# Four pieces of x on the scalar queue, six weight chunks loaded early into lent space, and high-part products first

## The chip, the cores and the metric

One NeuronCore of a Trainium2 chip runs the whole program in one launch. The metric is the device time of one execution in microseconds (us), as the median of several runs. Engines are named as the profile names them: PE is TensorE's matrix multiplication and PEld its weight load, DVE is VectorE, ACT is ScalarE, POOL is GpSimd, SP is SyncE, whose queue issues most of the transfers.

## What is computed

Two layers of a decoder trunk over 256 tokens of 1024 numbers, all in float32. Only the start of the first layer matters here:

```
def hybrid_layer(x, ...):
    h = rms_norm(x, attn_pre_gain)
    u = h @ w_in                      # 1024 -> 4120 columns
    qa, ka, va, qb, kcb, vcb, ksb, vsb, kwb, vwb, g_nsa, g_a, g_b = split(u)
    ...                               # two kinds of attention, merged
    x = x + rms_norm(mixed @ w_out, attn_post_gain)
    h = rms_norm(x, ffn_pre_gain)
    x = x + rms_norm(conv_ffn(h, ...), ffn_post_gain)
```

## The kernel before, in words

Every float32 matrix product is made of three products of a reduced type (float32r). A number is split into a high part (ScalarE copies and rounds it, `copy`, L114) and a low part (VectorE subtracts the high part from the number, `sub`, L117), and `mm3` (L365 to L368) multiplies high by high (L366), high of x by low of the weight (L367) and low of x by high of the weight (L368), all three into one PSUM bank. The row factor of the RMS norm is applied to the result, so products can run before it is known; the gain is multiplied into x.

The weights come as a stream of chunks in the order of their use (`Stream`, L145). `load` allots a staging tile `st`, of which there are four, and issues the transfer on SP's queue (L156, mostly 512 KB). `high` makes the high part `wh` on ScalarE and returns a function that makes the low part `wl` on VectorE; with that done the staging tile is free for the chunk after next. `next` hands the chunk out and makes those ahead of it.

The input projection `w_in` is cut into nine column tiles (`IN_TILES`), each with four chunks of 256 rows, so chunks 0 to 3 belong to tile 0, 4 to 7 to tile 1, and 8 to 11 to tile 2. A tile has two token halves (t = 0, 1) with a bank each, and `go(t, c)` does the six products of chunk c for one half. Tile 0 of layer 0 goes through its eight (t, c) pairs in the order of `FIRST`.

Before the first product x itself has to be prepared (`start`, L1111 on): `first_T(t, h)` transposes four 128 by 128 blocks of token half t and column half h on TensorE (L410) and multiplies by the gain on VectorE (L412); `first_split` makes high (ScalarE) and low (VectorE) parts of the result. `HOOKS` says before which of the eight pairs the other pieces of x and chunks 1 to 3 are prepared, and where the row sums of squares, the norm's factor and the rope's tables come (`rest`). `warm(n)` issues n products of zeros into a bank that nobody reads, six at the start and eight after the first transposes (`WARM`).

In this part, tile 0 of layer 0, TensorE, VectorE and ScalarE execute in the order in which the program is written (`MANUAL0`); after it a scheduler decides the order on each engine from dependences and its own costs. Every engine runs its queue in order. A transfer signals its landing on one of eight semaphores, used in turn, and the next transfer on the same semaphore is not issued before the previous one has landed.

At the start (L259 to L267) SP's queue gets the identity matrix (64 KB), the gain, chunk 0, the second column half of x's first token half (256 KB), chunk 1, all of x's second token half (512 KB), chunks 2 and 3; the scalar queue gets the first column half of x's first token half. Behind that SP issues positions, the other constants, the sinks and six small row loads (L281), then chunk 4.

Of the kernel before, what the change touches and what calls it, by code (L numbers as in the profile page):

```python
# [16 lines left out]
P = 128  # L17
# [33 lines left out]
MANUAL0 = {mybir.EngineType.PE, mybir.EngineType.DVE, mybir.EngineType.Activation}  # L51
PLAN = {'A': (23, 24, 24, 34), 'B0': (39, 43), 'B1': (49, 53, 58, 64), 'C': 66, 'S': (56, 75)}
DL = {'qa0': 2, 'qa1': 13, 'ka': 6, 'qb0': 8, 'qr0': 8, 'qb1': 2, 'qr1': 4, 'cb0': 1, 'cb1': 3, 'ks': 1, 'kw': 6, 'pT': (3, 3, 2), 'pv': 4, 'hT': 1, 'ge': 3, 'pj': 4, 'cT': 5, 'cv': 9, 'yT': 1, 'h0': 5, 'h1': 4, 'uf': 0, 'x0': 3, 'x1': 3}
WARM = (6, 8)
HOOKS = {0: '1C', 1: 'B2', 2: 'D', 6: '3r'}
FIRST = [(0, 0), (0, 1), (1, 0), (1, 1), (0, 2), (1, 2), (0, 3), (1, 3)]
CMPI = (0, 0, 0, 0, 4, 6, 7, 8)
AH = (2, 2, 2, 3, 2, 2, 2, 2, 2)
TG = True
# [6 lines left out]
def tile_hybrid_trunk(  # L66
# [21 lines left out]
    def nm(s):  # L88
        uid[0] += 1
        return f"{s}_{uid[0]}"  # L90
# [19 lines left out]
    def halves(ap):  # L110
        return [ap[:, 0:512], ap[:, 512:1024]]
# [33 lines left out]
    class Stream:  # L145
        def __init__(self):
            self.specs, self.loaded, self.made, self.used, self.front = [], {}, {}, 0, 0

        def add(self, src, a, b, tag="w", ahead=2):
            self.specs.append((src, a, b, tag, ahead))  # L150
# [1 line left out]

        def load(self, i):
            src, a, b, tag, _ = self.specs[i]
            st = wp.tile([P, a, b], F32, tag="st", bufs=4, name=nm("st"))
            nc.sync.dma_start(st, src)  # L156
            self.loaded[i] = st, a, b, tag

        def make(self, i=None):
            i = self.front if i is None else i  # L160
# [96 lines left out]
    pool.memset(rows, 0.0)  # L257
    grow = k1()[0:KD, 0:P]
    nc.sync.dma_start(cst[:, 0:P], consts[:, 0:P])  # L259
    act.dma_start(halves(X[:, 0, :])[0], halves(xv[:, 0, :])[0])  # L260
    nc.sync.dma_start(grow, attn_pre_gain[0].rearrange("(k p) -> k p", p=P))
    W.load(0)
    nc.sync.dma_start(halves(X[:, 0, :])[1], halves(xv[:, 0, :])[1])
    W.load(1)
    nc.sync.dma_start(X[:, 1, :], xv[:, 1, :])
    W.load(2)
    W.load(3)  # L267
    last_sq = [None]

    def table(fn):  # L270
# [15 lines left out]
    nc.sync.dma_start(cst[:, P:], consts[:, P:])  # L286
    sink = cp.tile([P, DEPTH, 8], F32, name="sink")
    nc.sync.dma_start(sink, attn_sinks.partition_broadcast(P))
    row_load(R_B1, cmp_b1.rearrange("l k h -> (l k) h"))
    row_load(R_POS, cmp_pos_emb.rearrange("l k (pr two) d -> (l k pr) (two d)", two=2))  # L290

# [123 lines left out]
    def first_split(t, h, m, pair):  # L415
        tk = slice(t * P, (t + 1) * P)
        ho = pair[0][:, h * 4:h * 4 + 4, tk]
        copy(ho, m)
        return lambda: sub(pair[1][:, h * 4:h * 4 + 4, tk], m, r32(ho))

    def attn_layer(l, xp, rs, gains, first):
# [2 lines left out]
        SG = [ap_.tile([P, QKV], F32, tag="sg", bufs=2, name=nm("SG")) for _ in range(2)]  # L424
        done = set()

        def in_tile(i, tag, fin, tmajor=False, hooks={}):
            c0, w = IN_TILES[i]
            bk = [bank(tag) for _ in range(2)]
            chs = {}  # L430

            def go(t, c):
                if c not in chs:
                    chs[c] = W.next(2, w)
                ch = chs[c]
                tk = slice(t * P, (t + 1) * P)
                for k in range(2):
                    kk = 2 * c + k
                    mm3(bk[t][:, :w], xh[:, kk, tk], xl[:, kk, tk], ch[0][:, k, :], ch[1][:, k, :], kk == 0, kk == 7)
                if c == 3:  # L440
                    fin(t, bk[t])
                if tmajor and t == 1 and c < 2:
                    W.make()

            order = FIRST if first and i == 0 else [(t, c) for t in range(2) for c in range(4)] if tmajor else [(t, c) for c in range(4) for t in range(2)]
            for t, c in order:
                for fn in hooks.get((t, c), ()):
                    fn()
                part(lambda: go(t, c))
# [661 lines left out]
    def start():  # L1111
        z = k2(F32R)
        dve.memset(r32(z), 0.0)
        zb = bank("S")

        def warm(n):
            for _ in range(n):
                pe.matmul(zb, z[:, 0:P], z, start=True, stop=True, skip_group_check=True)

        warm(WARM[0])  # L1120
        gb = bank("T")
        pe.transpose(gb[:, 0:KD], grow, ident[0:KD, 0:KD])
        dve.tensor_copy(gfirst, gb[:, 0:KD])
        low = first_split(0, 0, first_T(0, 0), xp)
        warm(WARM[1])
        lw = W.high(0)
        low()
        lw()

        def xs(*args):  # L1130
            lows = [first_split(t, h, first_T(t, h), xp) for t, h in args]
            for f in lows:
                f()

        def rest():
            for t in range(2):
                rs[t] = rstd_of(mean_sq(halves(X[:, t, :])))
            dve.tensor_scalar(nsink, sink, -1.0, None, ALU.mult)
            rope_tables()
        act_ = {"B": lambda: xs((0, 1)), "C": lambda: xs((1, 0)), "D": lambda: xs((1, 1)), "X": lambda: xs((1, 0), (1, 1)),  # L1140
                "1": lambda: W.make(1), "2": lambda: W.make(2), "3": lambda: W.make(3), "r": rest, "w": lambda: warm(3)}
        return {FIRST[i]: [act_[c] for c in h] for i, h in HOOKS.items()}

    more_rows()
    later(20, lambda: load_vec(0, 4))
# [84 lines left out]
```

## Time and profile before

| | |
|---|---|
| median of three runs | 800.55 us (799.91 to 801.0) |
| the profiled execution's own time | 800.75 us |
| its span, first to last instruction | 798.9 us |
| TensorE busy | 767.3 us (96%) |
| VectorE busy | 620.1 us (78%) |
| ScalarE busy | 497.7 us (62%) |
| GpSimd busy | 44.2 us (6%) |
| mean granted clock of TensorE | 0.991 of full |

The span is what the profile sees of the execution; 1.85 us of the execution's time lie outside it. Busy shares are means over stages with different limits. A busy TensorE is one with a product under way. The granted clock has two levels here, 1.0 and 0.5 of full, so that a mean tells what share of a stretch was spent at which. Times in the rows are us from the start of the span. In a timeline row stand start, duration, engine, line, operation, out<-in by names, shapes and the number of merged instructions, and in brackets the idle time before it and what ended it.

### The profile page before, as it was taken

How to read it: one execution, taken by the hardware profiler on the slowest of the kernel's cores; microseconds unless marked ns; L12 is line 12 of the kernel's file. 1: busy time of each engine (PE TensorE's matmuls, PEld its weight loads, DVE VectorE, ACT ScalarE, POOL GpSimd, SP SyncE). 2: the span in 40 equal slices, each digit the busy share in tenths (PEclk: the TensorE clock that was granted, in tenths of full speed). 3: DMA queues.
4: the chain of work that ended last, by engine and by line, in shares of the span. 5: the costliest groups of instructions: out<-in, count | busy, mean ns of one | idle time of the engine just before them, and what ended most of it. 6: DMA issues, size and time to landing. Idle time of an engine off the chain costs nothing.

```text
span 798.9 us, 13019 instructions
## 1 busy us (share of the span) xinstructions
PE 767.3 (96%) x4745; PEld 681.5 (85%) x4745; DVE 620.1 (78%) x1280; ACT 497.7 (62%) x952; POOL 44.2 (6%) x97
## 2 busy tenths in 40 slices
PE   7989989999899999999989999899998999999996
PEld 6778878888689999999968888888877999999995
DVE  5888888867768777777789999786867877767775
ACT  4678787755656555565555879667555655556552
POOL 2200022100200000000010000120001000000000
PEclk9998999999999999999999999999999999999998
DMA  7632156446556565665535232543545655656631
GB/s 266 226 100 89 61 155 202 133 162 182 191 177 186 185 185 186 207 216 185 182 106 179 90 119 78 196 162 132 187 156 170 199 185 185 185 185 210 213 106 53
DMA packets 42203, 131.26 MB, mean 164 GB/s; under 512 B 5359, under 2 KB 5915, under 8 KB 42139
## 3 DMA queue, kind: packets, MB, share of 16 engines
q1 hardware_dynamic: 41995, 130.18, 50.3%
q8 instruction: 37, 0.61, 0.3%
q10 hardware_dynamic: 144, 0.26, 0.1%
q14 instruction: 27, 0.22, 0.1%
HBM read 129.37 MB, written 1.05 MB: 163 GB/s over the span
## 4 chain that ended last, share of the span: by engine, by line
PE 81%; DVE 7%; ACT 6%; POOL 2%; issue 2%; DMA 1%; SPq 0%; DVEq 0%; POOLq 0%; ACTq 0%
PE mm L366 6%; PE mm L368 6%; PE mm L367 6%; PE S L367 5%; PE S L368 5%; PE S L366 5%; PE T L994 5%; PE T L993 5%; PE mm L994 5%; PE mm L993 5%; PE T L992 5%; PE mm L992 5%; PE O L366 3%; PE O L367 3%; PE O L368 3%; DVE wl L117 2%
## 5 line engine op out<-in xcount | busy, mean ns | idle before, releaser
L117 DVE TENSOR_TENSOR wl<-st,wh 128x1024 fp32r<-128x1024 f32 (+2 forms) x226 | 267.9, 1187 | 103.7 <-ACT wh L114 102.6
L114 ACT ACTIVATE wh<-st 128x1024 fp32r<-128x1024 f32 (+2 forms) x226 | 232.2, 1030 | 176.9 <-PE T L993 38.8
L366 PE MATMUL mm<-wh,x 128*128 128x512 f32 (+2 forms) x256 | 98.2, 384 | 3.4 <-DVE VT L508 2.4
L367 PE MATMUL mm<-wl,x 128*128 128x512 f32 (+2 forms) x256 | 95.8, 374 | 0.0
L368 PE MATMUL mm<-wh,x 128*128 128x512 f32 (+2 forms) x256 | 95.4, 373 | 0.1
L993 PE MATMUL mm<-q,wh 128*128 128x256 f32 x320 | 90.7, 283 | 0.0
L994 PE MATMUL T<-q,wl 128*128 128x256 f32 x320 | 90.6, 283 | 0.0
L993 PE MATMUL T<-q,wh 128*128 128x256 f32 x320 | 90.5, 283 | 0.0
L994 PE MATMUL mm<-q,wl 128*128 128x256 f32 x320 | 90.5, 283 | 0.0
L992 PE MATMUL T<-q,wh 128*128 128x256 f32 x320 | 90.5, 283 | 0.0
L992 PE MATMUL mm<-q,wh 128*128 128x256 f32 x320 | 90.5, 283 | 0.0
L992 PEld LDWEIGHTS mm<-q,wh 128*128 128x128 f32 x320 | 61.3, 192 | 0.9
L993 PEld LDWEIGHTS mm<-q,wh 128*128 128x128 f32 x320 | 61.3, 192 | 0.8
L992 PEld LDWEIGHTS T<-q,wh 128*128 128x128 f32 x320 | 61.3, 192 | 0.8
L993 PEld LDWEIGHTS T<-q,wh 128*128 128x128 f32 x320 | 61.3, 192 | 0.7
L994 PEld LDWEIGHTS mm<-q,wl 128*128 128x128 f32 x320 | 61.3, 192 | 0.1
L994 PEld LDWEIGHTS T<-q,wl 128*128 128x128 f32 x320 | 61.3, 192 | 0.0
L366 PEld LDWEIGHTS mm<-wh,x 128*128 128x128 f32 x256 | 49.5, 193 | 9.4 <-DVE VT L508 2.8
L368 PEld LDWEIGHTS mm<-wh,x 128*128 128x128 f32 x256 | 49.1, 192 | 6.6 <-DVE x L117 0.5
L367 PEld LDWEIGHTS mm<-wl,x 128*128 128x128 f32 x256 | 49.3, 193 | 5.2 <-DVE wl L117 0.4
L600 ACT ACTIVATE k<-k,mn 128x128 f32<-128x128 f32 (+1 forms) x96 | 42.6, 448 | 6.6 <-DVE mn L597 6.5
L114 ACT ACTIVATE k<-k 128x256 fp32r<-128x256 f32 x72 | 29.8, 414 | 10.8 <-DVE k L1005 5.8
(293 smaller groups left out, 1663.9 us busy)
## 6 DMA issues: line engine op xcount, KB each, us to landing
st<-in_ffn_w_up_dram SPq DMA_DIRECT2D x88, 512.0 KB, 4.2
st<-in_w_in_dram SPq DMA_DIRECT2D x48, 512.0 KB, 3.7
st<-in_ffn_w_down_dram SPq DMA_DIRECT2D x44, 512.0 KB, 3.7
st<-in_w_out_dram SPq DMA_DIRECT2D x16, 512.0 KB, 4.0
st<-in_w_in_dram SPq DMA_DIRECT2D x16, 384.0 KB, 3.2
st<-in_cmp_w_dram SPq DMA_DIRECT2D x16, 256.0 KB, 2.7
st<-in_w_branch_a_dram SPq DMA_DIRECT2D x8, 512.0 KB, 3.5
st<-in_w_branch_b_dram SPq DMA_DIRECT2D x8, 512.0 KB, 3.5
```

The source lines that it names most:

```text
L114: act.activation(dst, src, AF.Copy, scale=scale)
L117: dve.tensor_tensor(dst, a, b, ALU.subtract)
L366: pe.matmul(o, xh, wh, start=first, stop=False, skip_group_check=True)
L367: pe.matmul(o, xh, wl, start=False, stop=False, skip_group_check=True)
L368: pe.matmul(o, xl, wh, start=False, stop=last, skip_group_check=True)
L600: last_exp[0] = act.activation(self.pt[:, hh, s, :], sm[:, :nk], AF.Exp, bias=self.mn[:, i:i + 1], scale=-1.0, accum_out=self.dn[:, i:i + 1])
L992: pe.matmul(o, wh[:, k, :], hh[:, k, c0:c1], start=(k == 0), stop=False, skip_group_check=True)
L993: pe.matmul(o, wh[:, k, :], hl[:, k, c0:c1], start=False, stop=False, skip_group_check=True)
L994: pe.matmul(o, wl[:, k, :], hh[:, k, c0:c1], start=False, stop=(k == 7), skip_group_check=True)
```

## The change

Four things change, all in the program's first part.

- x is loaded in four pieces of 256 KB, all issued on the scalar queue, first the first column half of both token halves, then the second. SP's queue starts with constants, gain and chunks 0 to 3 in a row.
- Chunks 4 to 9 (tiles 1 and half of 2) are issued right behind the small constants, without waiting for staging tiles. `early` takes space that is used later: chunks 4 to 7 lie in the two tiles of the merge gates (`sg`), chunks 8 and 9 in the key tile (`kB`). The row loads stand behind them.
- For chunks 0 and 1 of tile 0 the 24 products are ordered by parts (`products`): for chunk 0 high by high for both token halves, then with wl, then with xl; for chunk 1 for each half high, xl, wl. `FIRST` goes over both token halves of a chunk before the next, and the preparation in `start` is written out in that order, with both first quarters of x transposed before the first product.
- The warm-up behind the first transposes has four products, not eight.

```
-WARM = (6, 8)
-HOOKS = {0: '1C', 1: 'B2', 2: 'D', 6: '3r'}
-FIRST = [(0, 0), (0, 1), (1, 0), (1, 1), (0, 2), (1, 2), (0, 3), (1, 3)]
+WARM = (6, 4)
+FIRST = [(0, 0), (1, 0), (0, 1), (1, 1), (0, 2), (1, 2), (0, 3), (1, 3)]
+EARLY = {4: ("sg", 2), 6: ("sg", 2), 8: ("kB", 1)}
...
         def load(self, i):
             src, a, b, tag, _ = self.specs[i]
-            st = wp.tile([P, a, b], F32, tag="st", bufs=4, name=nm("st"))
+            st = self.room.pop(i, None)
+            if st is None:
+                st = wp.tile([P, a, b], F32, tag="st", bufs=4, name=nm("st"))
             nc.sync.dma_start(st, src)
...
+        def early(self, i, tag, bufs):
+            both = ap_.tile([P, 2, 2, 512], F32, tag=tag, bufs=bufs, name=nm("early"))
+            self.room[i], self.room[i + 1] = both[:, 0], both[:, 1]
...
     nc.sync.dma_start(cst[:, 0:P], consts[:, 0:P])
-    act.dma_start(halves(X[:, 0, :])[0], halves(xv[:, 0, :])[0])
     nc.sync.dma_start(grow, attn_pre_gain[0].rearrange("(k p) -> k p", p=P))
-    W.load(0)
-    nc.sync.dma_start(halves(X[:, 0, :])[1], halves(xv[:, 0, :])[1])
-    W.load(1)
-    nc.sync.dma_start(X[:, 1, :], xv[:, 1, :])
-    W.load(2)
-    W.load(3)
+    for h in range(2):
+        for t in range(2):
+            act.dma_start(halves(X[:, t, :])[h], halves(xv[:, t, :])[h])
+    for i in range(4):
+        W.load(i)
...
+    for i, (tag, bufs) in EARLY.items():
+        W.early(i, tag, bufs)
+        W.load(i)
+        W.load(i + 1)
     row_load(R_B1, cmp_b1.rearrange("l k h -> (l k) h"))
...
+        def products(t, c, bk, chs, w):
+            todo = [(tt, p, k) for p in ((0, 0), (0, 1), (1, 0)) for tt in range(2) for k in range(2)] if c == 0 else \
+                   [(t, p, k) for p in ((0, 0), (1, 0), (0, 1)) for k in range(2)]
+            if c == 0:
+                todo = todo[6 * t:6 * t + 6]
+            for tt, (xp_, wp_), k in todo:
+                tk = slice(tt * P, (tt + 1) * P)
+                pe.matmul(bk[tt][:, :w], (xh, xl)[xp_][:, 2 * c + k, tk], chs[c][wp_][:, k, :],
+                          start=(c == k == xp_ == wp_ == 0), stop=False, skip_group_check=True)
...
+                if first and i == 0 and c < 2:
+                    products(t, c, bk, chs, w)
+                    return
...
-        low = first_split(0, 0, first_T(0, 0), xp)
+        m0 = first_T(0, 0)
+        lw0 = W.high(0)
+        low0 = first_split(0, 0, m0, xp)
+        low1 = first_split(1, 0, first_T(1, 0), xp)
         warm(WARM[1])
-        lw = W.high(0)
-        low()
-        lw()
-
-        def xs(*args):
-            lows = [first_split(t, h, first_T(t, h), xp) for t, h in args]
+        lw0()
+        low0()
+        low1()
+        W.make(1)
+
+        def second():
+            m0, m1 = first_T(0, 1), first_T(1, 1)
+            lw = W.high(2)
+            lows = [first_split(t, 1, m, xp) for t, m in ((0, m0), (1, m1))]
+            lw()
             for f in lows:
                 f()
...
+        steps = {2: [second], 4: [lambda: W.make(3)], 5: [rest]}
+        return {FIRST[i]: fns for i, fns in steps.items()}
```

TensorE at the start of the program, before the change (S is the bank of the warm-up, T a transpose, mm a bank of tile 0, x_8 and x_9 the high and low parts of x):

```order
L1118 MATMUL S_130<-k_61_128 128x512 x6
L1122 MATMUL T_137<-cst,k_2_76 128x8
L410 MATMUL T_140<-cst,X 128x128 x4
L1118 MATMUL S_130<-k_61_128 128x512 x8
L410 MATMUL T_167<-cst,X 128x128 x4
L366 MATMUL mm_161<-wh_156,x_8_110 128x512
L367 MATMUL mm_161<-wl_157,x_8_110 128x512
L368 MATMUL mm_161<-wh_156,x_9_111 128x512
```

The same place with the change (mm_180 and mm_181 are the banks of the two token halves, x_11 and x_12 high and low parts of x):

```order
L1142 MATMUL S_140<-k_64_138 128x512 x6
L1146 MATMUL T_147<-cst,k_2_76 128x8
L420 MATMUL T_150<-cst,X 128x128 x4
L420 MATMUL T_161<-cst,X 128x128 x4
L1142 MATMUL S_140<-k_64_138 128x512 x4
L445 MATMUL mm_180<-wh_157,x_11_120 128x512 x2
L445 MATMUL mm_181<-wh_157,x_11_120 128x512 x2
L445 MATMUL mm_180<-wl_158,x_11_120 128x512 x2
L445 MATMUL mm_181<-wl_158,x_11_120 128x512 x2
L445 MATMUL mm_180<-wh_157,x_12_121 128x512 x2
L445 MATMUL mm_181<-wh_157,x_12_121 128x512 x2
L420 MATMUL T_194<-cst,X 128x128 x4
```

The second quarter's transposes moved ahead of the warm-up, the first products are sorted by parts, and the other two quarters are transposed after twelve products.

SP's queue behind the loads of chunks 0 to 3, before (the four st tiles in a row are chunks 4 to 7):

```order
L288 DMA sink<-in_attn_sinks_dram 128x16
L281 DMA k_1_72<-in_cmp_b_dram 4x128
L281 DMA k_1_72<-in_cmp_pos_emb_dram 64x128
L281 DMA k_1_72<-in_ffn_conv_w_dram 128x128 x2
L281 DMA k_1_72<-in_ffn_conv_w_dram 8x128
L281 DMA k_1_72<-in_ffn_conv_b_dram 88x128
L156 DMA st_333<-in_w_in_dram 128x1024
L156 DMA st_357<-in_w_in_dram 128x1024
L156 DMA st_363<-in_w_in_dram 128x1024
L156 DMA st_369<-in_w_in_dram 128x1024
```

And with the change (st_469 is chunk 10):

```order
L294 DMA sink<-in_attn_sinks_dram 128x16
L159 DMA early_98<-in_w_in_dram 128x1024 x2
L159 DMA early_101<-in_w_in_dram 128x1024 x2
L159 DMA early_104<-in_w_in_dram 128x1024 x2
L287 DMA k_1_72<-in_cmp_b_dram 4x128
L287 DMA k_1_72<-in_cmp_pos_emb_dram 64x128
L287 DMA k_1_72<-in_ffn_conv_w_dram 128x128 x2
L287 DMA k_1_72<-in_ffn_conv_w_dram 8x128
L287 DMA k_1_72<-in_ffn_conv_b_dram 88x128
L159 DMA st_469<-in_w_in_dram 128x1024
```

Six chunks stand ahead of the row loads now.

VectorE between the tables of the rope (L339 to L342) and the first rope (L461, L463), before (wl_336 and wl_360 are the low parts of chunks 4 and 5):

```order
L339 SCALAR_TENSOR_TENSOR k_89_255<-k_89_255 128x64 x3
L340 TENSOR_SCALAR k_89_255<-k_89_255 128x64
L341 SCALAR_TENSOR_TENSOR k_89_255<-k_89_255 128x64
L342 TENSOR_SCALAR k_89_255<-k_89_255 128x64
L117 TENSOR_TENSOR wl_336<-st_333,wh_335 128x1024
L461 SCALAR_TENSOR_TENSOR k_90_282<-mm_161,rstd_242,tab 128x256
L463 SCALAR_TENSOR_TENSOR k_91_283<-mm_161,rstd_242,tab 128x4x32 x2
L117 TENSOR_TENSOR wl_360<-st_357,wh_359 128x1024
```

And with the change (wl_340, wl_362, wl_366 and wl_370 are chunks 4 to 7):

```order
L349 SCALAR_TENSOR_TENSOR k_92_255<-k_92_255 128x64 x3
L117 TENSOR_TENSOR wl_340<-early_98,wh_339 128x1024
L350 TENSOR_SCALAR k_92_255<-k_92_255 128x64
L117 TENSOR_TENSOR wl_362<-early_98,wh_361 128x1024
L351 SCALAR_TENSOR_TENSOR k_92_255<-k_92_255 128x64
L117 TENSOR_TENSOR wl_366<-early_101,wh_365 128x1024
L352 TENSOR_SCALAR k_92_255<-k_92_255 128x64
L117 TENSOR_TENSOR wl_370<-early_101,wh_369 128x1024
L485 SCALAR_TENSOR_TENSOR k_93_288<-mm_180,rstd_242,tab 128x256
```

Four splits stand ahead of the first rope instead of one. Behind that, the scheduler's order differs in places through the first layer's attention up to some 100 us, and is the same from there on.

## Rows read from the trace of the kernel before

**Rows 1.** The page, part 1: busy us, share of the span and instructions.

```profile
PE 767.3 (96%) x4745; PEld 681.5 (85%) x4745; DVE 620.1 (78%) x1280; ACT 497.7 (62%) x952; POOL 44.2 (6%) x97
```

**Rows 2.** Timeline of the start, all engines, 0 to 24 us.

```profile
1.44 2.93 PE L1118 MATMUL S<-k 128*128 128x512 f32 x6 [1.44 <-DVE k L1113]
...
4.92 1.12 PE L410 MATMUL T<-cst,X 128*128 128x128 f32 x4
...
5.69 2.33 PE L1118 MATMUL S<-k 128*128 128x512 f32 x8
...
6.80 0.63 ACT L114 ACTIVATE x<-k 128x512 fp32r<-128x512 f32 x1 [4.15 <-DVE k L412]
7.34 1.04 ACT L114 ACTIVATE wh<-st 128x1024 fp32r<-128x1024 f32 x1
7.46 0.69 DVE L117 TENSOR_TENSOR x<-k,x 128x512 fp32r<-128x512 f32 x1 [0.70 <-ACT x L114]
...
8.41 1.23 DVE L117 TENSOR_TENSOR wl<-st,wh 128x1024 fp32r<-128x1024 f32 x1 [0.25 <-ACT wh L114]
...
10.78 0.63 PE L410 MATMUL T<-cst,X 128*128 128x128 f32 x4 [2.76 <-DMA X<-in_x_dram]
...
11.17 0.48 PE L366 MATMUL mm<-wh,x 128*128 128x512 f32 x1
...
22.92 0.40 PE L367 MATMUL mm<-wl,x 128*128 128x512 f32 x1
...
23.15 0.39 PE L368 MATMUL mm<-wh,x 128*128 128x512 f32 x1
```

**Rows 3.** Timeline, 20 to 30 us: stops of TensorE for wl, and the first rope.

```profile
20.71 0.19 PEld L367 LDWEIGHTS mm<-wl,x 128*128 128x128 f32 x1 [0.36 <-DVE wl L117]
...
24.41 0.50 PE L367 MATMUL S<-wl,x 128*128 128x512 f32 x1 [0.41 <-DVE wl L117]
...
26.18 0.48 DVE L461 SCALAR_TENSOR_TENSOR k<-mm,rstd,tab 128x256 f32<-128x256 f32 x1 [1.82 <-POOL tab L348]
...
28.37 0.50 PE L367 MATMUL S<-wl,x 128*128 128x512 f32 x1 [1.16 <-DVE wl L117]
```

**Rows 4.** Timeline of SP's queue: issues of transfers, 0 to 15 us.

```profile
1.57 0.36 SPq L156 DMA_DIRECT2D st<-in_w_in_dram  x1
...
2.44 0.43 SPq L156 DMA_DIRECT2D st<-in_w_in_dram  x1
2.92 0.43 SPq L265 DMA_DIRECT2D X<-in_x_dram  x1
...
8.08 0.27 SPq L281 DMA_DIRECT2D k<-in_cmp_b_dram  x1
...
14.21 6.81 SPq L156 DMA_DIRECT2D st<-in_w_in_dram  x4
```

**Rows 5.** DMA issues at 1.57, 2.44 and 2.92: engine, count, KB, us to landing.

```profile
st<-in_w_in_dram SPq DMA_DIRECT2D x1, 512.0 KB, 4.2
...
st<-in_w_in_dram SPq DMA_DIRECT2D x1, 512.0 KB, 6.9
...
X<-in_x_dram SPq DMA_DIRECT2D x1, 512.0 KB, 7.7
```

**Rows 6.** Waits of SP's queue, 0 to 120 us: us in total, times, longest.

```profile
SPq L156 <- DVE wl L117: 60.6, 16, 17.6
...
SPq L281 <- DMA X<-in_x_dram: 1.7, 2, 1.0
```

**Rows 7.** Table by stretches: us, busy us of each engine, granted clock, DMA share, GB/s.

```profile
2.00:4.00 2.00, 2.00 (x6) 1.32 (x4) 0.00 (x0) 0.64 (x2) 2.00 (x3) 1.00 0.78 284
4.00:6.00 2.00, 1.61 (x7) 1.26 (x7) 0.79 (x2) 0.00 (x0) 1.45 (x3) 1.00 0.97 230
8.00:10.00 2.00, 0.02 (x1) 0.00 (x0) 1.38 (x2) 0.98 (x2) 0.00 (x0) 1.00 1.04 420
45.00:70.00 25.00, 21.29 (x134) 19.41 (x133) 19.65 (x88) 17.71 (x57) 0.00 (x0) 0.86 0.20 70
```

More of the change, by code (lines that the diff above doesn't have):

```diff
@@ L147, in __init__ @@
             self.specs, self.loaded, self.made, self.used, self.front = [], {}, {}, 0, 0
+            self.room = {}
         def add(self, src, a, b, tag="w", ahead=2):
@@ L1139, in rest @@
             rope_tables()
-        act_ = {"B": lambda: xs((0, 1)), "C": lambda: xs((1, 0)), "D": lambda: xs((1, 1)), "X": lambda: xs((1, 0), (1, 1)),
-                "1": lambda: W.make(1), "2": lambda: W.make(2), "3": lambda: W.make(3), "r": rest, "w": lambda: warm(3)}
-        return {FIRST[i]: [act_[c] for c in h] for i, h in HOOKS.items()}
+        steps = {2: [second], 4: [lambda: W.make(3)], 5: [rest]}
+        return {FIRST[i]: fns for i, fns in steps.items()}
     more_rows()
```

## The prediction

> **What bounds the kernel now.** I read the page first: TensorE is busy for 96% of the span [rows 1], so a gain has to come out of the 4% in which it waits or out of stretches at the lower clock. The timeline of the start shows the first such place. TensorE transposes the first quarter of x (128 tokens by 512 columns) at 4.92, runs eight warm-up products, and then sits idle for 2.76 us, until 10.78, before it can transpose x's second token half; the first real product starts at 11.17, although the split of chunk 0 that it needs was over at 9.64 (8.41 + 1.23) [rows 2]. From there products start 0.23 us apart, and the last of tile 0's 48 starts at 23.15, so tile 0 is over at about 23.4 [rows 2]. Read on for a few us and TensorE stops three more times for a low part of a weight chunk (wl): 0.36 us at 20.71, still in tile 0, then 0.41 and 1.16 us in tile 1 [rows 3]. The last of these is the rope's: VectorE had stood still for 1.82 us until 26.18, waiting for GpSimd's rope table, with the split of chunk 5 queued behind the rope [rows 3].
>
> The DMA view comes next. Chunk 0, chunk 1 and x's second token half, issued at 1.57, 2.44 and 2.92 [rows 4], landed 4.2, 6.9 and 7.7 us after that [rows 5], so at 5.8, 9.3 and 10.6. Chunk 4 is issued at 14.21 only [rows 4], and later chunks wait for a staging tile: the SP queue waited 60.6 us in 16 waits for low parts [rows 6].
>
> **The start, step by step.** I count KB landed against time. Landed are 832 KB (constants 64, first quarter of x 256, chunk 0 512) at 5.8, 1600 at 9.3 and 2112 at 10.6: the last 512 KB took 1.3 us, and at 420 GB/s from 8 to 10 us [rows 7] the engines look full. In the new order two queues share. What the first products need is the constants, two quarters of x and chunk 0: 1088 KB. A straight line between the first two points gives 7.0 us. Measured is the issue at 8.08 [rows 4], one of those that had to wait for a piece of x [rows 6]: the piece before chunk 1, with which just these 1088 KB are in. I take 8.0, as it is measured. The ends are 5.8, where the second quarter rides beside chunk 0 for nothing, and 10.0, where it falls behind chunk 1 (1856 KB: 9.3 and 256 KB more).
>
> A page speaks about this step. The Trainium skill, "DMA: Bandwidth & Descriptors", section "Rules for kernel authors", says that spreading transfers over issuing engines gives no bandwidth, because all of them run on the same 16 DMA engines and interleave; only issue time is saved. The trace agrees: with both queues at work the window from 2 to 4 us moved 284 GB/s, less than one queue did later [rows 7]. Were the scalar queue a path of its own, the second quarter would cost chunk 0 nothing and the first product could start at 5.8 + 1.04 + 0.63 = 7.5; by the rule it is 9.7, below.
>
> From 8.0 on, with the durations of now [rows 2]: ScalarE converts chunk 0 (1.04), then the first quarter of x (0.63), so the first product starts at 9.7. TensorE meanwhile has one group of transposes (0.63) and four warm-ups at 0.29 each, done at 9.8. VectorE has wl of chunk 0 at 10.3 (9.05 + 1.23) and the low parts of x (xl) at 11.0 and 11.7 (0.69 each). This is the point of the new order: four products of high parts run while wl is still made, then four with wl (from 10.6), then four with xl (from 11.5, 0.2 before the second is there, and two run ahead of it). Afterwards come two groups of transposes, as now, and 36 products. I carried those through in the same way. Chunk 1 lands at 10.0 (1856 KB), its wl is ready at 12.9 and wanted at 14.1; the second half of x and chunk 2 land at 11.9 (2624 KB), its xl is ready at 16.5 and wanted then; chunk 3 lands at 13.2, its wl is ready at 18.4 and wanted at 19.0. So nothing in tile 0 waits longer than a tenth, though with little slack, and the wait of 0.36 goes too. Against now that is 11.17 - 9.7 + 0.36 = **1.8 us**; tile 0 ends at 21.6. The four warm-ups dropped are worth nothing, as they run inside the wait for x.
>
> **The early chunks.** An issue on SP can wait for an older transfer to land, as the row loads do now [rows 6]. So chunk 4 is issued when the third quarter of x is in, near 9, and lands behind chunk 3 and the other constants at 15.2; chunks 5 to 9 follow every 1.3 us to 21.7. The six row loads and chunk 10 are pushed behind 3 MB. The rows are first read 20 parts of the program later, and chunk 10 is due in tile 2, so I cost that at nothing; with the cover gone it is one transfer, 1.3 us. The space lent to the chunks (merge-gate tiles, key tile) is written from tile 2 on, after their splits: nothing. Behind four squares ScalarE has the conversions one after the other, and VectorE now splits chunks 4 to 7 ahead of the first rope. Now 3.7 us lie between the ends of the splits of chunks 3 and 4, as the stops that they end show (20.71 and 24.41) [rows 3]; in the new order the split of chunk 4 comes before the last three of the small table operations, so at most 3.7 after 18.4, at 22.1, and I take 21.5, with those three at some 0.2 each (an estimate); it is wanted at 21.8. That of chunk 5 follows 1.4 later, at 22.9, and is wanted at 24.6. So both stops of tile 1 go: 0.41 + 1.16 = **1.6 us** [rows 3]. Bounds: 1.2, if the first stop stays, or none, if the rope still holds the second; all of it at best.
>
> **From tile 2 on** the scheduler puts instructions in another order, as far as the first 100 us go. Between 45 and 70 us TensorE is idle for 3.7 us (25 less 21.29), and the granted clock averages 0.86 there, which is 3.5 us of full clock [rows 7]. VectorE no longer loses its 1.82 us, so it comes to this stretch a little ahead. Bounds: both go, 7.2 us gained, or one more stop like the longest of now, 2.8 lost. I take 0.7 gained, near nothing, since the engines waited for are themselves busy for 19.65 and 17.71 of these 25 us [rows 7].
>
> **Sum.** 1.8 + 1.6 + 0.7 = 4.1 us. The profiled execution took 800.75 us (span 798.9 and 1.85 around it), so 796.65; the median of the three runs is 0.2 lower than that execution, so I forecast **796.4 us**.
>
> **Rivals.**
> *x comes sooner.* Between 4 and 6 us only 230 GB/s moved [rows 7]. If that hole belongs to the old queue order and does not return, the second quarter and chunk 0 land at 7.0 or earlier, and tile 0 gains another 1 to 1.7 us; with a shorter stretch at the lower clock later, 793.0 to 794.5. For it: the hole is unexplained. Against: rows of both queues still share the engines.
>
> *Half clock at the start.* TensorE will stand idle from about 6.0 to 8.0, with four warm-ups behind that and not eight ahead of it. The first six warm-ups took 2.93 us, 0.49 each, the later eight 2.33, 0.29 each [rows 2]: though the table's clock column says 1.00 there [rows 7], it starts at the lower level (1.2 GHz) and was raised during its early work. At 45 to 70 it fell back for some time [rows 7]. A stretch of that kind over the first products costs half to all of 3.5 us: 798.1 to 799.9. Against: 2.76 us of idleness at 8 were followed by products 0.23 apart [rows 2]. The Trainium skill, "TensorE: Matmul & The Clock Gate", section "Part 1: The HAM clock gate", has half rate as the default, which activity lifts and idleness restores; the rows at 45 to 70 agree, the idle time at 8 does not show it.
>
> *The shift is absorbed.* If ScalarE and VectorE, not TensorE, set when layer 0's attention ends, the gain becomes a wait there: about 1 us is left, 799 to 800. For it: how busy both are from 45 on [rows 7]. Against: their work there hangs on TensorE's products and starts earlier with them.
>
> *Slower: x behind the weights.* If the engines favour SP's rows, the second quarter lands at 10.0 or later. TensorE's queue is in order, so the transposes hold back even products that could run: transposes to 10.6, warm-ups to 11.8, where the first product stood at 11.17, so 0.6 lost less the 0.36. The idle time before is then 4 us, and a half-clock stretch behind it costs 3.5 more: 3.7 lost, 1.6 won back in tile 1, the 0.7 not gained: 2.1 slower, 802.6. It decides from a landing of about 10 us together with the lower clock. For it: the rows of SP's packets are twice as long. Against: now the first quarter, on the scalar queue, was transposed at 4.92, before chunk 0 had landed [rows 2, 5].
>
> **How the numbers follow.** A measurement of this kernel can tell 0.2%, 1.6 us, from no change; the borders are 798.95 and 802.15. Chances: forecast 0.62 (794.5 to 798.1), x sooner 0.08, half clock at the start 0.13, absorbed 0.12, slower 0.05. Faster: the first two, half of the half-clock case and a little of the absorbed one, 0.79; slower 0.05; within, the rest, 0.16. The range goes from 793.0, x sooner, to 799.2, which takes in half of the half-clock case; the rest of that, the slower case and most of the absorbed one lie outside, just under 2 in 10.
>
> **What would show it.** Right: the first product near 9.7, tile 0 over near 21.6, no wait for wl in tile 1, chunks 4 to 9 landed by 22, and all work at 120 us 3 to 5 us earlier. Wrong: the second quarter's transposes after 9, products 0.46 apart in the first 15 us, a rope that still holds a split back on VectorE, or a stretch between 45 and 100 us that gives the shift back. The timeline, the table by stretches and the granted clock tell these apart.

## The result and the profile after

| | before | after |
|---|---|---|
| median | 800.61 us (799.91 to 801.0, 4 runs) | 796.05 us (795.82 to 796.29, 4 runs) |
| ratio, 95% interval | | 0.9944 (0.9927 to 0.9961) |
| the profiled execution | 800.75 us, span 798.9 | 796.12 us, span 794.3 |

The change is faster by 4.6 us; 796.4 was forecast, 793.0 to 799.2 the range. The parts of the sum came out otherwise. Two executions that ran slow throughout, one of 1060.58 us in the run of the kernel before with its tables on ScalarE and one of 1241.54 us of the kernel before beside the last run (granted clock 0.653 and 0.557), are left out of the times below. TensorE is as busy as it was (767.3 us before [rows 1]):

```profile
PE 766.1 (96%) x4741; PEld 681.0 (86%) x4741; DVE 619.5 (78%) x1280; ACT 497.1 (63%) x952; POOL 47.2 (6%) x97
```

TensorE's timeline in tiles 0 and 1, after the change (start, duration, engine, line, operation, and in brackets the idle time before it); it answers to [rows 2, 3]:

```profile
1.44 2.93 PE L1142 MATMUL S<-k 128*128 128x512 f32 x6 [1.44 <-DVE k L1137]
4.84 0.24 PE L1146 MATMUL T<-cst,k 8*128 8x8 f32 x1 [0.48 <-DMA k<-in_attn_pre_gain_dram]
5.01 1.97 PE L420 MATMUL T<-cst,X 128*128 128x128 f32 x8
6.63 2.06 PE L1142 MATMUL S<-k 128*128 128x512 f32 x4
8.49 1.91 PE L445 MATMUL mm<-wh,x 128*128 128x512 f32 x4
10.19 1.27 PE L445 MATMUL mm<-wl,x 128*128 128x512 f32 x4
...
21.08 0.39 PE L378 MATMUL mm<-wh,x 128*128 128x512 f32 x1
...
29.47 0.50 PE L496 MATMUL T<-ident_r,k 128*128 128x128 f32 x4 [1.66 <-DVE k L117]
...
34.23 0.39 PE L378 MATMUL S<-wh,x 128*128 128x512 f32 x1
```

Both first quarters of x are transposed without a break at 5.01, so the wait of 2.76 us is gone. The first product starts at 8.49, not 11.17, but four warm-ups take 2.06 us and the first four products are some 0.43 apart, where 0.23 is the full pace: half clock until about 10.6. That is read from the spacing; the column of the granted clock gives 1.00 from 6 to 12 us here. Tile 0's last product starts at 21.08 (23.15 before). In tile 1 no stop for wl is left. In their place stands one that was not there: the transposes of the first rope wait 1.66 us, until 29.47. Tile 1 ends at 34.23; before it was

```profile
36.84 0.39 PE L368 MATMUL S<-wh,x 128*128 128x512 f32 x1
```

so of the 2.07 us gained in tile 0, tile 1 adds only 0.54. The new stop's origin, in the timelines of VectorE, GpSimd and ScalarE (the cosine, L354) after the change:

```profile
19.36 1.22 DVE L117 TENSOR_TENSOR wl<-early,wh 128x1024 fp32r<-128x1024 f32 x1
...
23.15 1.21 DVE L117 TENSOR_TENSOR wl<-early,wh 128x1024 fp32r<-128x1024 f32 x1
25.95 0.48 DVE L485 SCALAR_TENSOR_TENSOR k<-mm,rstd,tab 128x256 f32<-128x256 f32 x1 [1.60 <-POOL tab L358]
...
17.90 0.58 POOL L365 TENSOR_TENSOR rstd<-rstd,neg_half 128x1 f32<-128x1 f32 x1
...
19.36 1.64 POOL L365 TENSOR_TENSOR rstd<-rstd,neg_half 128x1 f32<-128x1 f32 x1
...
21.87 3.39 POOL L359 TENSOR_SCALAR tab<-k 128x64 f32<-128x64 f32 x4
25.23 1.35 POOL L358 TENSOR_SCALAR tab<-k 128x64 f32<-128x64 f32 x4
...
23.26 0.26 ACT L354 ACTIVATE k<-k 128x64 f32<-128x64 f32 x1 [0.64 <-DVE k L352]
```

VectorE now splits four chunks almost without a pause from 19.36 to 24.36. In that time the same GpSimd operations are slow: the norm's factor (L365) takes 1.64 us where it had taken 0.58, and the first four table operations 0.85 us each where the last four, with VectorE standing, take 0.34. At 0.34 throughout, the last four could have begun when the cosine was there (23.26 + 0.26), not at 25.23: 1.7 us sooner, an estimate from these rows. The transposes of the rope stand behind 28 of tile 1's 48 products in TensorE's queue, and there TensorE waits for them.

Most of the rest comes between 45 and 65 us. Table by stretches (us, busy us of each engine, granted clock, DMA share, GB/s), before:

```profile
45.00:57.00 12.00, 10.28 (x69) 8.61 (x67) 10.13 (x42) 8.09 (x20) 0.00 (x0) 1.00 0.28 99
57.00:65.00 8.00, 6.64 (x33) 6.63 (x34) 5.25 (x25) 4.62 (x17) 0.00 (x0) 0.57 0.00 0
```

and after:

```profile
45.00:57.00 12.00, 9.29 (x61) 7.79 (x61) 11.12 (x48) 9.29 (x21) 0.00 (x0) 0.91 0.38 133
57.00:65.00 8.00, 8.00 (x58) 7.70 (x57) 6.50 (x31) 6.13 (x29) 0.00 (x0) 0.92 0.00 0
```

Full clock lost is 8 x 0.43 = 3.4 us before, and 12 x 0.09 + 8 x 0.08 = 1.7 after; TensorE's idle time is 3.1 and 2.7 us. Together that is some 2.1 us more; the sum is rough, as idle time at the lower clock is counted in both. The first product of 384 columns, which comes behind this stretch, before and after:

```profile
92.36 0.44 PE L366 MATMUL mm<-wh,x 128*128 128x384 f32 x1
...
87.65 0.44 PE L376 MATMUL mm<-wh,x 128*128 128x384 f32 x1
```

There the lead is 4.7 us, and the two spans differ by 4.6.

### The profile page after: what moved, and what is told of

It reads as the page before. It is cut to its first block, busy times and chain, and to the rows that moved or that the text cites. A ratio compares the mean times of both kernels' runs of the same rounds, so it can differ in the third digit from the quotient of the medians.

```text
span 794.3 us, 13013 instructions
## 1 busy us (share of the span) xinstructions
PE 766.1 (96%) x4741; PEld 681.0 (86%) x4741; DVE 619.5 (78%) x1280; ACT 497.1 (63%) x952; POOL 47.2 (6%) x97
## 4 chain that ended last, share of the span: by engine, by line
PE 80%; DVE 8%; ACT 7%; POOL 3%; issue 2%; DMA 0%; DVEq 0%; POOLq 0%; SPq 0%; ACTq 0%
PE mm L376 6%; PE mm L377 6%; PE mm L378 6%; PE S L377 5%; PE S L378 5%; PE S L376 5%; PE T L1018 5%; PE T L1017 5%; PE mm L1018 5%; PE mm L1017 5%; PE T L1016 5%; PE mm L1016 5%; PE O L376 3%; PE O L377 3%; PE O L378 3%; DVE wl L117 2%
## 5 line engine op out<-in xcount | busy, mean ns | idle before, releaser
L117 DVE TENSOR_TENSOR wl<-st,wh 128x1024 fp32r<-128x1024 f32 (+2 forms) x220 | 260.5, 1186 | 102.2 <-ACT wh L114 100.9
L114 ACT ACTIVATE wh<-st 128x1024 fp32r<-128x1024 f32 (+2 forms) x220 | 226.0, 1030 | 176.8 <-PE O L378 38.7
L376 PE MATMUL mm<-wh,x 128*128 128x512 f32 (+2 forms) x248 | 94.1, 380 | 0.1
L377 PE MATMUL mm<-wl,x 128*128 128x512 f32 (+2 forms) x248 | 92.3, 372 | 0.0
L378 PE MATMUL mm<-wh,x 128*128 128x512 f32 (+2 forms) x248 | 92.0, 371 | 0.0
L376 PEld LDWEIGHTS mm<-wh,x 128*128 128x128 f32 x248 | 47.6, 192 | 5.6 <-ACT k L114 0.4
L378 PEld LDWEIGHTS mm<-wh,x 128*128 128x128 f32 x248 | 47.2, 190 | 5.9
L377 PEld LDWEIGHTS mm<-wl,x 128*128 128x128 f32 x248 | 47.5, 192 | 4.8
L364 POOL TENSOR_SCALAR rstd<-s 128x1 f32<-128x1 f32 x16 | 6.6, 412 | 518.2 <-ACT k L372 518.1
```

The costliest lines, as they stand in the source:

```text
L114: act.activation(dst, src, AF.Copy, scale=scale)
L117: dve.tensor_tensor(dst, a, b, ALU.subtract)
L364: pool.tensor_scalar(r, s2[:, 0:1], s2[:, 1:2], EPS, ALU.add, ALU.add)
L376: pe.matmul(o, xh, wh, start=first, stop=False, skip_group_check=True)
L377: pe.matmul(o, xh, wl, start=False, stop=False, skip_group_check=True)
L378: pe.matmul(o, xl, wh, start=False, stop=last, skip_group_check=True)
```

## The experiments

Diffs are against the changed kernel unless said otherwise. A kernel's start differs from one execution to the next (first below), so single landmarks are compared only between profiles with like starts.

**The changed kernel again.** No edit.

> The changed kernel once more, unchanged, beside the runs below on the same chip. Theory A (the start differs from run to run in when chunk 0 lands and when the clock rises, as 8.49 here against 7.72 and 7.84 in two kernels with the same loads shows): first product anywhere from 7.7 to 8.5, tile 0 over from 19.6 to 21.1, the stop for the rope at its 1.6 us wherever tile 0 stands, total 795.2 to 796.5. Rival B (the start of the profiled run is fixed, and the others were faster through their edits): first product at 8.5 again.

Measured: 795.44 us (794.4 to 796.25), ratio to before 0.9933 (0.9918 to 0.9949). TensorE's timeline of this execution:

```profile
4.30 0.27 PE L1146 MATMUL T<-cst,k 8*128 8x8 f32 x1
...
6.12 1.67 PE L1142 MATMUL S<-k 128*128 128x512 f32 x4
7.81 1.25 PE L445 MATMUL mm<-wh,x 128*128 128x512 f32 x4
...
19.57 0.39 PE L378 MATMUL mm<-wh,x 128*128 128x512 f32 x1
...
32.76 0.39 PE L378 MATMUL S<-wh,x 128*128 128x512 f32 x1
```

Theory A. Here the gain's 4 KB were there in time, the products run 0.27 apart from the first, and tile 0 is over 1.5 us sooner. From tile 0 to tile 1 it is 13.19 us, against 13.15 in the first profile: the stop for the rope stays, wherever tile 0 ends. Of the 1.5 us between the two executions at the end of tile 0, 0.7 is left in their times.

**x loaded as before.**

```
-    for h in range(2):
-        for t in range(2):
-            act.dma_start(halves(X[:, t, :])[h], halves(xv[:, t, :])[h])
-    for i in range(4):
-        W.load(i)
+    act.dma_start(halves(X[:, 0, :])[0], halves(xv[:, 0, :])[0])
+    W.load(0)
+    nc.sync.dma_start(halves(X[:, 0, :])[1], halves(xv[:, 0, :])[1])
+    W.load(1)
+    nc.sync.dma_start(X[:, 1, :], xv[:, 1, :])
+    W.load(2)
+    W.load(3)
```

> The changed kernel with x loaded as before: first quarter on the scalar queue, the other pieces on SP between the chunks, x's second token half whole behind chunk 1. All else as changed. Theory A (the order of the loads makes the gain at the start): first product at 11 to 12.5, tile 0 over 2 to 4 us later, total 798 to 800. Rival B (with the wait of 4 us the lower clock stays as well): 800 to 803. Rival C (the order of the preparation and of the products makes the gain, not the loads): within 0.7 of the changed kernel.

Measured: 802.18 us (800.71 to 804.63), ratio 1.0018 (1.0004 to 1.0032). TensorE's timeline:

```profile
4.69 0.68 PE L422 MATMUL T<-cst,X 128*128 128x128 f32 x4
10.89 1.09 PE L422 MATMUL T<-cst,X 128*128 128x128 f32 x4 [5.52 <-DMA X<-in_x_dram]
11.63 2.06 PE L1144 MATMUL S<-k 128*128 128x512 f32 x4
13.49 1.05 PE L447 MATMUL mm<-wh,x 128*128 128x512 f32 x2
```

Theory B: a wait of 5.52 us, warm-ups and products at half clock behind it, the first product at 13.49. This is the prediction's slower rival brought about by an edit, and its price (802.6) was nearly right. Without the new loads the rest of the change is a loss of some 1.5 us, so the gain cannot be had without them: the transposes of both token halves now stand ahead of the first product in TensorE's queue, and it hangs on when the second half lands. That the loads alone would do, with the preparation and the products in their old order, is not shown; no run has that.

**Three of x's pieces on SP's queue.**

```
-    for h in range(2):
-        for t in range(2):
-            act.dma_start(halves(X[:, t, :])[h], halves(xv[:, t, :])[h])
-    for i in range(4):
+    act.dma_start(halves(X[:, 0, :])[0], halves(xv[:, 0, :])[0])
+    nc.sync.dma_start(halves(X[:, 1, :])[0], halves(xv[:, 1, :])[0])
+    W.load(0)
+    for t in range(2):
+        nc.sync.dma_start(halves(X[:, t, :])[1], halves(xv[:, t, :])[1])
+    for i in range(1, 4):
         W.load(i)
```

> x in four pieces in the same order, but three of them on SP's queue: the second quarter ahead of chunk 0, the other two between chunks 0 and 1. Theory A (all transfers share the same engines, only order and bytes count): the first product within 0.5 us of 8.49, total 795.5 to 796.7. Rival B (the scalar queue as a second path brought x forward): the first product at 9.2 or later, total 796.7 to 798.

Measured: 795.22 us (794.8 to 795.79), ratio 0.9929 (0.9909 to 0.9948), the first product at 8.34. Theory A by its numbers, but they do not show that the queue counts for nothing. The gain's 4 KB were in time here, so the like start is the one with 7.81, and the first product is 0.5 later than there. And the scheduler's order differs in tile 1: the rope's transposes stand behind 37 products and not 28, TensorE's stop for them is 0.41 us, and from tile 0 (20.42) to tile 1 (32.32) it is 11.90 us. That gain is lost again behind it, where from 45 to 57 the clock is 0.75 (0.91 in the changed kernel):

```profile
29.61 0.51 PE L498 MATMUL T<-ident_r,k 128*128 128x128 f32 x4 [0.41 <-DVE k L117]
...
45.00:57.00 12.00, 9.14 (x56) 8.11 (x56) 11.13 (x47) 9.99 (x27) 0.00 (x0) 0.75 0.37 129
```

On the bytes A does not hold. From 4 to 6 us, in this kernel:

```profile
4.00:6.00 2.00, 2.00 (x9) 1.68 (x9) 1.17 (x3) 0.00 (x0) 1.45 (x3) 1.00 0.96 311
```

and in the changed kernel:

```profile
4.00:6.00 2.00, 1.52 (x7) 1.17 (x7) 0.69 (x2) 0.10 (x1) 1.45 (x3) 1.00 0.99 384
```

With x loaded as before it was 255, and 230 in the kernel before [rows 7]: the new order fills part of that hole and the second queue another part. The next 2 us moved 336 and 397.

**The old order of products** (`if False:` for the branch that calls `products`; only tile 0's order on TensorE differs).

> The changed kernel with the products of chunks 0 and 1 in the old order, high by high, wl, xl for each block. Theory A (the order saves time while wl and xl are made, but the later stop for the rope, which does not hang on these products, absorbs what is lost here): tile 0 ends 0.5 to 1.3 us later, the stop at 29.5 shrinks by as much, total 796.0 to 796.6. Rival B (nothing absorbs it): total 796.6 to 797.4. Rival C (at the lower clock the parts are ready anyway): tile 0 ends within 0.3 us, total as changed.

Measured: 796.1 us (795.17 to 796.45), ratio 0.9938 (0.9918 to 0.9957). Its first product starts at 7.72 and tile 0's last at 20.34, against 7.81 and 19.57 in the second profile of the changed kernel: 0.8 lost while wl and xl are made, as both A and B have it; C falls. The total lies 0.05 above the first measurement of the changed kernel and 0.66 above the second, so it doesn't tell A from B. But tile 1 takes 13.13 us here too, so its stop absorbed nothing, which speaks against A.

**Eight warm-ups behind the first transposes** (`WARM = (6, 8)`).

> The changed kernel with eight warm-up products behind the first transposes and not four. Theory A (they lie in TensorE's wait for the split of chunk 0): within 0.3 of the changed kernel beside it. Rival B (at the lower clock they take 0.46 us each and push the first product back): 0.5 to 1.5 above it. Rival C (they lift the clock sooner and steady the start): 0.4 to 1.0 below it.

Measured: 795.74 us (794.5 to 797.43), 0.3 above the changed kernel beside it: A, as far as the spread tells. In the profiled execution, the slowest of the six and one of the late starts, they take 3.08 us and the first product starts only at 9.65: there they do push it back.

**No early chunks** (`EARLY = {}`).

> The changed kernel without the early chunks: chunk 4 and those after it wait for staging tiles again, everything else as changed. Theory A (the early chunks only swapped one stop for another: the stops for wl in tile 1 went, 1.6 us, and a stop of 1.66 us for the rope came): the stops for wl come back, the stop for the rope goes, tile 1 ends within 0.5 us of the changed kernel, total 796.0 to 797.0. Rival B (the term of the prediction, 1.6 us, is real and the rope's stop has another cause): 797.3 to 799.

Measured: 795.82 us (795.17 to 797.37), ratio 0.9939 (0.9917 to 0.9961). Theory A, nearly. The norm's factor on GpSimd, the first rope on VectorE and TensorE's stops in tile 1:

```profile
18.54 0.56 POOL L365 TENSOR_TENSOR rstd<-rstd,neg_half 128x1 f32<-128x1 f32 x1
...
22.10 0.48 DVE L485 SCALAR_TENSOR_TENSOR k<-mm,rstd,tab 128x256 f32<-128x256 f32 x1 [1.62 <-POOL tab L358]
...
24.29 0.50 PE L377 MATMUL S<-wl,x 128*128 128x512 f32 x1 [0.67 <-DVE wl L117]
...
27.32 0.51 PE L496 MATMUL T<-ident_r,k 128*128 128x128 f32 x4 [0.70 <-DVE k L117]
```

One stop for wl of 0.7 us is back, the stop for the rope shrinks from 1.7 to 0.7, and tile 0 to tile 1 is again 13.14 us. The early chunks only swapped one stop for another. VectorE waits for GpSimd's table as long as before, 1.62 us, though the factor is no longer held up: the table is late without the early splits too.

**The rope's tables on ScalarE.**

```
-                pool.tensor_scalar(tab[:, i, :, dd], c, f, None, ALU.mult)
-                pool.tensor_scalar(tab[:, i + 1, :, dd], s, g, None, ALU.mult)
+                copy(tab[:, i, :, dd], c, scale=f)
+                copy(tab[:, i + 1, :, dd], s, scale=g)
```

> The changed kernel with the eight operations of the rope's tables on ScalarE and not on GpSimd. Theory A (GpSimd's table operations are held up by VectorE's splits that the early chunks brought together, and so make the rope late): VectorE's stop of 1.60 us and TensorE's of 1.66 us at 29.5 go or shrink below 0.4, tile 1 ends 1.2 to 1.7 us earlier, total 794.2 to 795.2. Rival B (the rope is late because four splits stand in front of it): the stop stays above 1 us, total 795.6 to 796.6.

Measured: 793.13 us (792.73 to 793.58), ratio 0.9902 (0.9883 to 0.9922). ScalarE, GpSimd and VectorE:

```profile
22.05 1.28 ACT L114 ACTIVATE tab<-k 128x64 f32<-128x64 f32 x8
...
17.89 1.65 POOL L365 TENSOR_TENSOR rstd<-rstd,neg_half 128x1 f32<-128x1 f32 x1
...
21.64 1.22 DVE L117 TENSOR_TENSOR wl<-early,wh 128x1024 fp32r<-128x1024 f32 x1
22.78 0.48 DVE L485 SCALAR_TENSOR_TENSOR k<-mm,rstd,tab 128x256 f32<-128x256 f32 x1
```

Theory A by its stops. All eight operations take 1.28 us, the rope follows the last split with no wait, and from tile 0 (19.63) to tile 1 (31.21) it is 11.58 us, 1.6 less. The four splits still stand in front of the rope, so B falls. The run takes the tables off GpSimd whole, so it does not tell what the splits add to their time from what GpSimd needs by itself. The total is 1.1 below what A allowed: of the 2.3 us to the changed kernel, 1.6 are the stop, and the rest lies behind tile 1.

**The kernel before with the tables on ScalarE** (the same edit there).

> The kernel before with the tables on ScalarE alone. Theory A (there GpSimd's table operations took 0.36 us each, hardly held up by splits, so only the handing over is saved): VectorE's stop of 1.82 us shrinks to 0.5 to 1.2, TensorE's stop of 1.16 us for wl with it, total 0.5 to 1.2 below the kernel before. Rival B (the late tables cost the kernel before as much as the changed one): 2.5 to 3.3 below it. Rival C (another instruction order behind it and the lower clock there swamp it): within 0.4 of it, or above.

Measured: 799.16 us (797.73 to 802.03, 11 executions), ratio 0.9988 (0.9971 to 1.0005), some 1 us below the kernel before: theory A by its size, though the interval takes in no difference. Its profile shows more than A had: VectorE's stop goes whole, both stops for wl go, and tile 0 to tile 1 is 12.60 us, not 13.69. Then TensorE stands still for 1.62 us until 57.40 for a copy on ScalarE; the longest stop of that kind in the kernel before is 0.69.

**Tables on ScalarE and no early chunks.**

> Tables on ScalarE as before, and in addition no early chunks. Theory A (the early chunks are worth the stops for wl that they remove as soon as the rope is not late; with the tables on GpSimd the rope's stop hid that): stops for wl of together 0.7 to 1.6 us in tile 1, total 793.8 to 794.8, against 793.13 with the early chunks. Rival B (early chunks are worth nothing in either case): 792.9 to 793.5.

Measured: 791.7 us (790.97 to 792.3), ratio 0.9886 (0.9868 to 0.9904): better than either theory, and below the lowest time with the early chunks, 792.73, in every execution. Tile 1 has no stop for wl at all, with the rope out of the way, and takes 11.54 us. With the tables on GpSimd it took 13.14 without early chunks, so the move is worth 1.6 us in tile 1 here as it is with them: the late tables do not come from the early chunks. In this kernel the stretch from 45 to 65 is at full clock:

```profile
45.00:57.00 12.00, 10.35 (x73) 8.72 (x72) 10.98 (x52) 9.96 (x28) 0.00 (x0) 1.00 0.14 45
57.00:65.00 8.00, 7.47 (x61) 7.43 (x62) 7.74 (x29) 7.86 (x26) 0.00 (x0) 1.00 0.17 66
```

One difference between the orders is plain. In the changed kernel, ScalarE and TensorE:

```profile
52.95 1.28 ACT L629 ACT_TABLE_LOAD   x1
54.24 0.21 ACT L629 ACTIVATE co<-co 128x4 f32<-128x4 f32 x1
54.35 0.40 ACT L114 ACTIVATE k<-k 128x256 fp32r<-128x256 f32 x1
...
54.80 0.30 PE L496 MATMUL T<-ident_r,k 128*128 128x128 f32 x1 [1.62 <-ACT k L114]
```

The scheduler put the exponential's table load ahead of a copy that TensorE waits for. In this run it stands behind that copy, and the wait is 0.27 us; either edit alone leaves the stop at 1.62 or 1.63. The next two runs ask whether that is the reason.

**The table load behind the exponentials.**

```
-                    act.activation(e[:, 0:4], e[:, 0:4], AF.Exp)
+                    with behind(last_exp[0] if first else None):
+                        act.activation(e[:, 0:4], e[:, 0:4], AF.Exp)
```

> The changed kernel, with the first activation on the sinks (L629), which brings the load of the exponential's table with it, issued behind the exponentials of its own unit in layer 0. Theory A (TensorE's stop of 1.62 us that ends at 54.80 is that load of 1.28 us standing in ScalarE's queue ahead of the copy that TensorE waits for, and the half clock behind it comes from the standing still): the stop goes, granted clock 1.00 from 45 to 65 or nearly, total 1.5 to 3.3 below the changed kernel, 792.2 to 794.0. Rival B (the scheduler puts another stop in its place, such as the one of 1.79 us for the values in the kernel before): within 0.7 of the changed kernel.

Measured: 795.76 us (795.46 to 797.82), ratio 0.9942 (0.9927 to 0.9956). TensorE's timeline:

```profile
52.20 0.28 PE L496 MATMUL T<-ident_r,k 128*128 128x128 f32 x1 [0.26 <-ACT k L114]
...
54.61 0.60 PE L376 MATMUL mm<-wh,x 128*128 128x280 f32 x1 [1.33 <-DVE VT L532]
```

Theory B. The stop of 1.62 goes, as A said, and 2 us on stands one of 1.33 for the values, with the clock at 0.82 and 0.84 in the two stretches: VectorE is the next to be late. (The profiled execution, 797.82 us, is the slowest of the six.)

**Both: tables on ScalarE, the load behind, early chunks kept.**

> Rope tables on ScalarE and the table load behind the exponentials, with the early chunks. Theory A (without the early chunks the same was 791.7 because the scheduler happened to put the table load behind the copies; the early chunks themselves cost nothing): 790.8 to 792.0. Rival B (the early chunks cost something of their own, such as work on ScalarE brought forward): 792.4 to 793.4, as with the tables on ScalarE alone.

Measured: 794.54 us (792.2 to 796.9), ratio 0.9919 (0.9901 to 0.9937). Neither: no better than with the tables alone, over a wide spread, with the same stop of 1.33 us for the values and a clock of 0.86 from 45 to 57. So the place of the table load is not enough to make the kernel as fast as the one without early chunks. The scheduler orders the whole stretch otherwise there; which part of that order counts is not settled.

**The best version: tables on ScalarE, no early chunks, eight warm-ups first** (`WARM = (8, 4)`).

> Tables on ScalarE, no early chunks, and eight warm-up products at the very start where there were six, so that TensorE does not stand idle when the gain's 4 KB land late. Theory A (where TensorE waited 0.48 to 0.80 us for the gain, the four warm-ups behind took 2.06 us, half clock, and where it did not wait they took 1.15 to 1.67; so filling that wait lifts the clock sooner): the four take 1.2 to 1.7 us, first product at 7.8 to 8.7, total 790.8 to 791.6, against 791.7 with six. Rival B (two more at 0.49 us each push the transposes and the first product back by what they take, and nothing is won): first product at 8.8 or later, total 791.8 to 792.6.

Measured: 790.58 us (790.42 to 791.97), ratio 0.9877 (0.9855 to 0.9899). TensorE's timeline:

```profile
1.44 3.78 PE L1142 MATMUL S<-k 128*128 128x512 f32 x8 [1.44 <-DVE k L1137]
5.15 0.27 PE L1146 MATMUL T<-cst,k 8*128 8x8 f32 x1
5.35 1.76 PE L420 MATMUL T<-cst,X 128*128 128x128 f32 x8
6.87 1.19 PE L1142 MATMUL S<-k 128*128 128x512 f32 x4
7.91 1.38 PE L445 MATMUL mm<-wh,x 128*128 128x512 f32 x4
```

Theory A: no wait, the later four warm-ups in 1.19 us, the first product at 7.91, the total 0.2 below its range. The 1.1 us against six warm-ups lie inside the two intervals, but the times of both kernels are below the changed kernel's lowest, 794.4, in every execution. This is the version to keep: some 10 us below the kernel before, twice what the change gained.

## Why the prediction was right, and where its terms were not

**The start, 1.8 forecast, 2.07 measured** (3.6 in the second profile). It needs the new loads, as the run with x loaded as before shows. The landing of 8.0 us was wrong: chunk 0, issued at 1.57, took

```profile
st<-in_w_in_dram SPq DMA_DIRECT2D x1, 512.0 KB, 5.0
```

and was in at 6.6, with both quarters of x ahead of it. The 8.0 was read off a row load that was issued at 8.08 in the old order of SP's queue, and even the straight line through the old landings (7.0) was too late, as it carried the hole of 230 GB/s along, and the hole went. So "x comes sooner" came true; "half clock at the start" came true beside it in the first profile, and the two nearly cancelled: the first product came 1.2 us before the forecast 9.7, and tile 0 was over at 21.3, where 21.6 was forecast. Products twice as far apart in the first 15 us were one of the prediction's own signs of being wrong. That the term came out all the same is luck. The Trainium skill, "DMA: Bandwidth & Descriptors", section "Rules for kernel authors", has no bandwidth to win from a second issuing engine; here 4 to 6 us moved 384 GB/s (387 in the second profile) with all of x on the scalar queue and 311 with three of its four pieces on SP's, so for this stretch the measurement says otherwise, though the total was the same.

**Tile 1, 1.6 forecast, 0.5 measured.** The splits came in time, and both stops for wl went (of the chunks, the last two took 7.7 us from their issue at about 12, so they landed by 20). The step that failed is the next one, "So both stops of tile 1 go: 0.41 + 1.16 = 1.6 us". It took the stops that go for time that is won, and put the rope's own way at nothing: four splits ahead of it, GpSimd's operations beside these splits, and its transposes at a fixed place in TensorE's queue. A stop of 1.66 us for them took the place of the two. The bound "none, if the rope still holds the second" is near by its size, but the split of chunk 5 stood ahead of the rope.

What makes that stop is shown in part. With the tables on ScalarE it goes, so the late table is needed for it. With three of x's pieces on SP's queue VectorE waits 1.59 us for the table all the same, but the transposes stand nine products further back and the stop is 0.41: their place is needed too. That a split holds GpSimd up is shown by the durations; that this makes the table late is not, since VectorE waits 1.62 us for it without the early splits as well.

**From tile 2 on, 0.7 forecast, 2.1 measured.** The place was right and the size too small. Of the 2.1 us, some 1.7 is the lower clock, which lasted half as long. No run sets this clock by itself, so its cause stays open. This term is a draw: the median of the kernel before was 800.50 to 801.55 beside the various runs, its single times 796.5 to 803.2, and its mean granted clock was 0.997 in the three fastest and 0.987 to 0.993 in those above 801. That the forecast came out within 0.4 us is luck in part: a miss of 1.1 down and one of 1.4 up nearly cancel.

**The rivals.** "Absorbed" did not happen: the lead grows behind 45 us. The slower one had its price about right, as the run with x loaded as before shows, and its condition wrong: with the new order of loads the second quarter is in before chunk 0.

## What to carry to other kernels

Load first what the head of the in-order queue needs, in pieces of the size in which it is used; without that the rest of this change was a loss. Before counting a removed stop as time won, cost the next late engine in the same stretch: the early chunks handed the wait from wl to the rope, and moving the table load handed it from ScalarE to VectorE. And look at what runs on the neighbour engine: a split that nobody waits for can stretch an operation that somebody does wait for.

## What the runs showed of the hardware

- A GpSimd operation beside VectorE's split of a chunk is held up: the one of 0.56 to 0.58 us took 1.64 and 1.65 when both started together, which is the split's 1.22 and another 0.4; the split's own time did not change. The Trainium skill, "SBUF — State Buffer", section "Who interferes with whom", states that a VectorE instruction with two inputs in SBUF contends with a GpSimd instruction that reads SBUF, over ports that one of the two holds at a time. The rows agree: the hold-up of some 1.1 us is nearly the split's whole length.
- How soon TensorE ran at its full pace at the start went with a transfer of 4 KB. In the three profiles with six and four warm-ups and x in the new order in which TensorE waited 0.48 to 0.80 us for the gain, the four warm-ups took 2.06 us; in the six with no such wait, or 0.24 us, they took 1.15 to 1.67. With eight first there was none. That the wait is the cause is likely, not shown: it could not be set by itself.
